# adaLN chunks of a two-layer diffusion block: transposes that end a chunk moved to later tiles, the steps of the first layer's chunks all on GpSimd, and the two value matmuls of a key tile made to wait for both their inputs

## The chip, the cores and the metric

The kernel runs on one core of one Trainium2 chip. The metric is the time of one execution on the device, in microseconds (us). Three timed runs of the kernel before gave 1271.01, 1266.54 and 1269.44 us, median 1269.44 us. One further execution was profiled, and all rows shown are from it.

## The reference, cut to what matters

Two layers work on 512 latent tokens of 1024 features (`h`); 256 context tokens feed the first layer's keys and values only. The first layer is windowed attention (16 heads of 64, 4 groups of keys and values, blocks of 128 queries, a sink per head), the second a short gated convolution. Each is followed by a feed-forward part (FFN) with a convolution over the tokens and 2816 hidden features. All is float32.

```
m = silu(c) @ ada_w[i] + ada_b[i]                 # (6 * 1024), per layer
sh1, sc1, g1, sh2, sc2, g2 = split(m, 6)
a = rms_norm(h) * (1 + sc1) + sh1
h = h + g1 * mixer(a)                             # layer 0: window attention, layer 1: gated conv
a = rms_norm(h) * (1 + sc2) + sh2
h = h + g2 * ((silu(conv(g)) * conv(u)) @ w_down) # g, u = split(a @ w_up, 2)
# attention, per head and block of 128 queries:
e = exp(s - max); o = (e @ v) / (sum(e) + exp(sink - max))
```

The six vectors of a layer are called chunks 0 to 5 here: shift, scale and gate of the mixer, then shift, scale and gate of the FFN.

## The kernel before, in words

Activations are held with features on the 128 rows, so `h` is 8 tiles of 128x512. Large products run as three matmuls in a reduced float32 format on a high and a low part of each operand (`mm3`, lines 168 to 171): each weight piece is loaded by SyncE's DMA queue (`wraw`, line 145), cast by ScalarE (line 137) and subtracted by VectorE (line 138).

**Order.** The code is written as one long sequence, and a scheduler that runs when the program is built turns it into one queue per engine (TensorE, VectorE, ScalarE, GpSimd) and one for SyncE's DMAs. It goes by the order of the code, but lets an instruction pass another one that it takes to be not yet ready; it works with its own estimates of durations. On the chip each queue is then worked off strictly in order. `tc.keep_in_program_order` keeps an instruction behind all that the code has put on its engine before it. Two hand-written lists give the order of the code: `START` up to the keys and values, `HEADS` for the attention.

**adaLN chunks.** Chunks 0 and 1 of layer 0 are computed at the start by TensorE. The others are computed in steps, `ada_step(layer, chunk, kt)`, off TensorE: a step loads 128 rows of `ada_w` as two halves of 128x512 (`araw`, 4 buffers) and adds them, times a column of silu(c), to two accumulators of 128x512 (`adaacc`, 2 buffers, the two halves of one chunk). After the eighth step (`kt` 7) the sum over the 128 rows is still to be taken: for each half, four transposes on TensorE into the bank `qt` (line 240), a reduction on VectorE (242) and the bias (243). In the attention the `a` steps of `HEADS` do chunks 2, 3, 4 of layer 0, one half of a step on VectorE (227, 229), the other on GpSimd (231, or 233 and 234). In layer 0's FFN, `tail0(j)` after each of the 22 tiles j does up to three steps, for chunk 5 of layer 0 and chunks 0 to 5 of layer 1, both halves on GpSimd.

**FFN of layer 0.** Tile j is two projections of 8 feature tiles (48 matmuls of 512 columns). After tiles 7, 15 and 21 the finished third is projected down (`out_proj`): 8 output tiles of 8, 8 or 6 hidden tiles, three matmuls each.

**Attention.** For a head and query block, `score` makes two or four matmuls, VectorE finds maxima and masks (line 552), ScalarE exponentiates (555). `value(p, j)` takes key tile j for the two heads of pair p: it transposes the weights of 2, 3 or 4 query blocks (583) into banks `pt` (3 of them), copies them out to `pf` (3 buffers; VectorE at 588 for context tiles, ScalarE at 590 for the others), and multiplies by the values (592). The even head's result goes to rows 0 to 63 of one bank, the odd head's to rows 64 to 127, each by its own matmul with 64 of the array's 128 columns; the profile lists each as two instructions. For key tiles 0 and 5, with two query blocks, both heads share one `pf` and one copy. `inverse_sums` (`r`) and `normalise` (`f`) finish a pair; the low part of the result is made on GpSimd (612).

GpSimd also adds the two halves of the rotary turn of keys and queries (line 435) and makes the scale of late queries (420, 421). Keys are transposed at line 467 once they are turned (430 to 435, 454).

Of the kernel before, what the change touches and what calls it, by code (L numbers as in the profile page):

```python
# [8 lines left out]
F32R = mybir.dt.float32r  # L9
AF = mybir.ActivationFunctionType  # L10
# [3 lines left out]
P = 128  # L14
T = 512
# [12 lines left out]
# Key tiles stand in the order lat0 lat1 ctx0 ctx1 lat2 lat3, so the keys of every query block are one window.  # L28
# [5 lines left out]
HOOK_AT = 6  # a norm's second half goes out after so many steps of the next phase's first group  # L34
HALF_AT = 2  # and its first half after so many tiles of the last phase's second half
KEY_BLOCKS = ((0, 2), (0, 3), (0, 4), (0, 4), (1, 4), (2, 4))

# Columns of the packed small parameters.
PC = {}
_n = 0  # L40
for _k, _w in (("c", 16), ("gmix", 16), ("adab", 2 * 6 * KT), ("gffn", 16), ("fconv", 2 * 3 * 2 * NF), ("sconv", 3 * KT),
# [6 lines left out]
# The order of the steps up to the keys and values: x, c, a, w, p load latents, context, a slice of ada_w, weights of k and v and the  # L48
# other parameters; r are the rstds, g a slice of silu(c) @ ada_w, s a split of weights, m and n the modulated features of latents and
# context, l and t their keys and values, k keeps the tensor engine's clock up while it waits.  # L50
# [4 lines left out]
# The order of the steps of the attention: q is a block of the second half of q, h the transposes of a pair of heads, s.b a head's scores  # L55
# of a query block, v.j a pair's values of a key tile, r its inverse sums, f its output, a a step of silu(c) @ ada_w, L and W weights.
HEADS = """
    q0 h0 a s0.0 s0.1 s0.3 s0.2 h1 s1.0 s1.1 s1.3 q2 a s1.2 s2.1 s2.3 s2.2 q1 v0.2 q3 v0.0 v0.3 s3.1 a h2 s2.0 a s3.0 s3.2 r0 v0.1
    a s3.3 v0.4 v0.5 f0 a s4.1 s4.0 s4.3 h3 v1.2 v1.3 a s4.2 s5.1 s5.0 a v1.0 s5.2 v1.1 s5.3 v1.4 v1.5 r1 a s6.0 s6.1 f1 s6.3 h4 a
    s6.2 v2.3 a v2.2 s7.0 a r2 s7.1 s7.3 s7.2 a v2.0 v2.1 v2.4 v2.5 s8.0 f2 a h5 s8.2 v3.3 s8.3 v3.0 s8.1 a s9.0 a s9.1 s9.3 v3.2  # L60
    v3.1 r3 a a s9.2 v3.4 s10.0 s10.1 s10.3 v3.5 s10.2 v4.2 f3 h6 v4.3 a v4.1 s11.0 s11.1 s11.3 s11.2 r4 s13.1 v4.0 v4.4 s12.3 a
    s12.2 a v4.5 f4 h7 a v5.3 v5.2 s12.0 s13.0 s12.1 a s13.3 v5.1 a v5.0 s13.2 v5.4 v5.5 r5 f5 s14.0 s14.3 s14.1 s14.2 L v6.2 v6.3
    s15.0 W s15.1 r6 s15.3 s15.2 v6.0 v6.1 v6.4 v6.5 v7.2 v7.3 v7.0 v7.1 r7 v7.4 f6 v7.5 f7
# [4 lines left out]
def kernel(ctx: ExitStack, tc: tile.TileContext, xT, ctxT, par_d, rope_d, mask_d, ident_d,  # L68
# [43 lines left out]
    # ---------------------------------------------------------------- constants  # L112
# [22 lines left out]
    # ---------------------------------------------------------------- helpers  # L135
# [12 lines left out]
    splits = [0, 0]  # so many splits in one piece, then so many in halves  # L148
# [33 lines left out]
    def rstd(acc, late=False, tag=None):  # L182
        """1 / sqrt(mean + EPS) of the tokens of acc (sums of squares by feature row), the same on all rows."""
        n = acc.shape[-1]
        nb = n // P
        ps = bank(tag) if tag else nbank()
        for b in range(nb):
            pe.matmul(out=ps[:, b:b + 1], lhsT=acc[:, b * P:(b + 1) * P], rhs=ones[:, 0:1], start=True, stop=True)
        c_ = small(NB, "rcol")[:, :nb]
        if late:  # L190
            vec.tensor_scalar(out=c_, in0=ps[:, :nb], scalar1=EPS, scalar2=None, op0=ALU.add)
            pool.tensor_tensor(out=c_, in0=c_, in1=mhalf[:, :nb], op=ALU.pow)
        else:
            act.activation(out=c_, in_=ps[:, :nb], func=AF.Sqrt, bias=epst, scale=1.0)
            vec.reciprocal(out=c_, in_=c_)
        ps = bank(tag) if tag else nbank()
        for b in range(nb):
            pe.transpose(out=ps[:, b * P:(b + 1) * P], in_=c_[:, b:b + 1].broadcast_to([P, P]), identity=ident)
        r = tmp()[:, :n]
        act.copy(out=r, in_=ps[:, :n])  # L200
        return r

    def modulate(x, r, s, sh, hi, lo):
        """hi + lo = x * s * r + sh."""
        n = tmp()[:, :x.shape[-1]]
        vec.scalar_tensor_tensor(out=n, in0=x, scalar=s, in1=r, op0=ALU.mult, op1=ALU.mult)
        act.activation(out=hi, in_=n, func=AF.Identity, scale=1.0, bias=sh)
        vec.scalar_tensor_tensor(out=lo, in0=n, scalar=sh, in1=hi.bitcast(F32), op0=ALU.add, op1=ALU.subtract)  # L208
# [3 lines left out]
    def ada_step(layer, ch, kt):  # L212
        """One of the KT steps of a chunk of silu(c) @ ada_w; the last one also leaves the chunk as columns."""
# [8 lines left out]
        for half in range(2):  # L222
            w, a = raws[half], acc[half]
            c_ = cs[:, kt, 0:1]
            if adastate["eng"][half] == "v":
                if kt == 0:
                    vec.tensor_scalar(out=a, in0=w, scalar1=c_, scalar2=None, op0=ALU.mult)
                else:
                    vec.scalar_tensor_tensor(out=a, in0=w, scalar=c_, in1=a, op0=ALU.mult, op1=ALU.add)
            elif kt == 0:  # L230
                pool.tensor_scalar(out=a, in0=w, scalar1=c_, scalar2=1.0, op0=ALU.mult, op1=ALU.mult)
            else:
                pool.tensor_scalar(out=w, in0=w, scalar1=c_, scalar2=1.0, op0=ALU.mult, op1=ALU.mult)  # L233
                pool.tensor_tensor(out=a, in0=a, in1=w, op=ALU.add)  # L234
        if kt < KT - 1:
            return
# [11 lines left out]
    # ---------------------------------------------------------------- layer 0: adaLN, norm, keys, values, queries  # L248
# [6 lines left out]
    with ExitStack() as attn:  # L255
# [22 lines left out]
        with tc.tile_pool(name="start", bufs=1, reuse_waits="tile") as st:  # L278
# [46 lines left out]
            def gemv(e):  # L325
                """Columns e*128.. of shift and scale for c and c_ctx: rows of partial sums side by side in the array, then columns."""
# [44 lines left out]
        adastate["eng"] = "vp"  # L371
        adastate["acc_alloc"] = lambda: ap.tile([P, 512], F32, tag="aacc", name=nm("adaacc"), bufs=2)
# [30 lines left out]
        def inv_rms(ss, out, scale, n):  # L403
            """out = scale / sqrt(ss / HD + EPS), the square root refined by one Newton step; n columns."""
# [10 lines left out]
        def inv_rms_late(ps, out):  # L415
            """Minus the above for 8 heads of q, without a change of the activation table."""
# [6 lines left out]
        def do_rope(src, tab, b, nh, out):  # L423
            """src [P, nh*HD] -> out, rotated by the gained tables of block b."""
# [33 lines left out]
        # keys transposed: KA holds k_hi on both halves of the rows, KB holds k_lo  # L458
# [46 lines left out]
        # ------------------------------------------------------------ window attention  # L505
# [9 lines left out]
        def head_pair(h):  # L515
            """q of heads h, h+1 transposed; each as a tile with q_hi on one half of the rows and q_lo on the other."""
# [15 lines left out]
        def score(h, b):  # L532
            """Unnormalised weights of head h for query block b; their sums go to den, after the last block the sinks' part to dsk."""
# [27 lines left out]
        def value(p, j):  # L561
            """Values of key tile j of heads 2p, 2p + 1, weighted, feature-major: the even head on rows 0.. of po, the odd on 64.."""
# [12 lines left out]
            for t in range(2):  # L575
# [9 lines left out]
                if t or not both:  # L585
                    w = 512 if both else n * P
                    if j in CTX_SLOT:
                        vec.tensor_copy(out=pf[:, :w], in_=pt[:, :w])
                    else:
                        act.copy(out=pf[:, :w], in_=pt[:, :w])  # L590
            for t in range(2):
                pe.matmul(out=po[t * HD:(t + 1) * HD, b0 * P:b1 * P], lhsT=V[:, j, kv, :], rhs=pfs[t], start=first, stop=not pair["left"])  # L592

        def inverse_sums(p):
            """1 / (den + dsk) of a pair of heads, spread over the rows of their values."""
# [4 lines left out]
            inv = ap.tile([P, 512], F32, tag="inv", name=nm("inv"), bufs=1)  # L600
# [3 lines left out]
            R = pairs[p]["R"] = ap.tile([P, 512], F32, tag="R", name=nm("R"), bufs=2)  # L604
# [9 lines left out]
        adastate["eng"] = "vp"  # L614
        for step in HEADS.split():
# [14 lines left out]
            elif k == "a":  # L630
                ada_step(*asteps.pop(0))
# [6 lines left out]
    # ---------------------------------------------------------------- the rest, feature-major  # L638
    with tc.tile_pool(name="ffn", bufs=1, reuse_waits="tile") as fp, three_banks() as sp3:
# [5 lines left out]
        adastate["acc_alloc"] = lambda: fp.tile([P, 512], F32, tag="aacc", name=nm("adaacc"), bufs=2)  # L645
# [10 lines left out]
        def proj(pieces, ah, al, halves=False, group=None, hook=None):  # L656
            """One bank for each weight piece; k-major over `group` pieces at a time. `hook` is called HOOK_AT steps in."""
# [37 lines left out]
        def out_proj(src, n, ah, al, gate, nxt=None, last=False, lead=(), tail_w=None):  # L695
            """h += gate * (W^T a). With `nxt`, h is final after it and the next norm follows half by half."""
# [33 lines left out]
        adastate["eng"] = "pp"  # L730
# [35 lines left out]
        fsteps = [(0, 5, kt) for kt in range(KT)] + [(1, ch, kt) for ch in range(6) for kt in range(KT)]  # L766

        def tail0(j):
            for _ in range(3 if j else 0):
                if fsteps:  # L770
                    ada_step(*fsteps.pop(0))

        def after_ffn0():
            assert not fsteps
# [7 lines left out]
        # layer 1: short gated convolution  # L782
# [88 lines left out]
```

## Time and profile before

| what | value |
|---|---|
| timed runs | 1271.01, 1266.54, 1269.44 us; median 1269.44 |
| profiled execution | span 1263.3 us; its own full time is not given, the median is 6.1 us above its span |
| TensorE busy | 1227.5 us, 97% |
| VectorE, ScalarE, GpSimd busy | 772.6, 490.3, 352.5 us |
| mean granted TensorE clock | 0.991 |
| start, to about 118 us | keys, values, first queries |
| attention | about 118 to 275 us |
| output projection and norm | about 275 to 325 us |
| FFN of layer 0 | about 325 to 682 us |
| layer 1 | about 682 to 1263 us |

How rows are read: DVE is VectorE, ACT ScalarE, POOL GpSimd, SP SyncE, PE a matmul and PEld the load of its weights. A row of a view names engine, line, operation, what is written from what is read, and a count. A row of a list of waits says how long an engine sat idle before instructions of a line, and whose end released it. In a timeline the columns are start and length in us, and in brackets the idle time before. Matmuls overlap: the time from one matmul's start to the next one's start tells more than a duration. A transpose is a matmul too.

### The profile page before, as it was taken

The page shows a single profiled execution, that of the slowest core. Times are in us where ns is not written, and L with a number is a line of the kernel's source. Part 1 is how long each engine was busy: PE and PEld are TensorE (multiplying, and loading weights), DVE is VectorE, ACT ScalarE, POOL GpSimd, SP SyncE. Part 2 cuts the span into 40 slices and gives each one's busy share as a digit, 9 for nine tenths or more (in the row PEclk, how much of TensorE's full clock was granted, in tenths as well). Part 3 has the DMA queues.
Part 4 walks back from the last instruction along what each step waited for, and adds up shares of the span by engine and source line. Part 5 has one row for each costly group of instructions (what it writes and reads, how often), then busy time and mean ns, then how long its engine had stood idle before and what let it go on. Part 6 is the DMA issues. An engine that isn't in the chain of part 4 may idle for free.

```text
span 1263.3 us, 16133 instructions
## 1 busy us (share of the span) xinstructions
PE 1227.5 (97%) x6190; PEld 986.5 (78%) x6190; DVE 772.6 (61%) x1157; ACT 490.3 (39%) x812; POOL 352.5 (28%) x301
## 2 busy tenths in 40 slices
PE   8989999999899999989999999999999999999998
PEld 6667655568887788777878998888988888888888
DVE  4789878735887637765575764443676436653652
ACT  4435666642463223331234442332454224432330
POOL 0054344209329928897280100001000000000000
PEclk8989999999999999989999999999999999999999
DMA  9454232035344554555342233222233233323211
GB/s 366 168 184 158 68 125 85 25 112 196 109 146 151 202 168 151 200 193 193 120 149 96 89 113 100 89 96 83 68 133 98 87 99 100 100 87 98 80 38 67
DMA packets 57741, 157.58 MB, mean 125 GB/s; under 512 B 6464, under 2 KB 8000, under 8 KB 57664
## 3 DMA queue, kind: packets, MB, share of 16 engines
q1 hardware_dynamic: 57664, 156.56, 37.6%
q8 instruction: 48, 0.79, 0.3%
q14 instruction: 29, 0.24, 0.1%
HBM read 152.86 MB, written 2.10 MB: 123 GB/s over the span
## 4 chain that ended last, share of the span: by engine, by line
PE 77%; POOL 13%; DVE 5%; issue 2%; DMA 1%; ACT 1%; SPq 0%; POOLq 0%; DVEq 0%; ACTq 0%
PE ps_s L170 8%; PE ps_s L169 8%; PE ps_s L171 8%; PE ps_pt L170 7%; PE ps_pt L171 7%; POOL adaacc L234 7%; PE ps_pt L169 7%; POOL araw L233 5%; PE ps_oa L592 5%; PE ps_oa L170 3%; PE ps_oa L169 3%; PE ps_oa L171 3%; PE ps_pt L583 3%; PE ps_qt L170 2%; PE ps_qt L171 2%; PE ps_qt L169 2%
## 5 line engine op out<-in xcount | busy, mean ns | idle before, releaser
L138 DVE TENSOR_TENSOR wlo<-wraw,whi 128x1024 fp32r<-128x1024 f32 (+2 forms) x206 | 246.0, 1202 | 165.1 <-ACT whi L137 160.3
L137 ACT CAST whi<-wraw 128x1024 fp32r<-128x1024 f32 (+2 forms) x206 | 195.9, 959 | 332.8 <-PE ps_s L170 98.6
L234 POOL TENSOR_TENSOR adaacc<-adaacc,araw 128x512 f32<-128x512 f32 x119 | 171.9, 1451 | 6.3
L170 PE MATMUL ps_s<-a,whi 128*128 128x512 f32 (+1 forms) x376 | 140.5, 374 | 2.6 <-DVE a L208 2.6
L169 PE MATMUL ps_s<-a,whi 128*128 128x512 f32 (+1 forms) x376 | 140.6, 374 | 0.0
L171 PE MATMUL ps_s<-a,wlo 128*128 128x512 f32 (+1 forms) x376 | 140.0, 372 | 0.0
L169 PE MATMUL ps_pt<-a,whi 128*128 128x512 f32 (+1 forms) x368 | 135.8, 369 | 0.0
L170 PE MATMUL ps_pt<-a,whi 128*128 128x512 f32 (+1 forms) x368 | 135.7, 369 | 0.0
L171 PE MATMUL ps_pt<-a,wlo 128*128 128x512 f32 (+1 forms) x368 | 135.1, 367 | 0.0
L233 POOL TENSOR_SCALAR araw<-araw,cs 128x512 f32<-128x512 f32 x119 | 117.7, 993 | 45.2 <-DMA araw<-in_ada 40.1
L137 ACT CAST g<-f 128x512 fp32r<-128x512 f32 x52 | 32.2, 620 | 141.4 <-DVE f L754 140.8
L170 PEld LDWEIGHTS ps_s<-a,whi 128*128 128x128 f32 x376 | 71.3, 190 | 14.8 <-DVE a L208 2.8
L169 PEld LDWEIGHTS ps_s<-a,whi 128*128 128x128 f32 x376 | 71.3, 190 | 12.3
L171 PEld LDWEIGHTS ps_s<-a,wlo 128*128 128x128 f32 x376 | 71.2, 189 | 12.2
L169 PE MATMUL ps_pt<-g,whi 128*128 128x512 f32 (+1 forms) x222 | 78.3, 353 | 1.2 <-ACT g L137 0.6
L169 PEld LDWEIGHTS ps_pt<-a,whi 128*128 128x128 f32 x368 | 69.8, 190 | 11.3
L171 PEld LDWEIGHTS ps_pt<-a,wlo 128*128 128x128 f32 x368 | 69.7, 189 | 11.1
L170 PE MATMUL ps_pt<-g,whi 128*128 128x512 f32 (+1 forms) x222 | 78.0, 352 | 0.2 <-DVE g L138 0.2
L170 PEld LDWEIGHTS ps_pt<-a,whi 128*128 128x128 f32 x368 | 69.7, 189 | 10.8
L171 PE MATMUL ps_pt<-g,wlo 128*128 128x512 f32 (+1 forms) x222 | 78.0, 352 | 0.0
L171 PE MATMUL ps_s<-g,wlo 128*128 128x512 f32 (+1 forms) x222 | 77.9, 352 | 0.0
L169 PE MATMUL ps_s<-g,whi 128*128 128x512 f32 (+1 forms) x222 | 77.7, 351 | 0.0
(258 smaller groups left out, 2489.7 us busy)
## 6 DMA issues: line engine op xcount, KB each, us to landing
wraw<-in_wup SPq DMA_DIRECT2D x88, 512.0 KB, 3.6
araw<-in_ada SPq DMA_DIRECT2D x160, 256.0 KB, 2.9
wraw<-in_wdown SPq DMA_DIRECT2D x32, 512.0 KB, 3.9
wraw<-in_wsc SPq DMA_DIRECT2D x24, 512.0 KB, 3.6
gw<-in_ada SPq DMA_DIRECT2D x16, 512.0 KB, 9.9
wraw<-in_wqkv SPq DMA_DIRECT2D x12, 512.0 KB, 6.8
wraw<-in_wdown SPq DMA_DIRECT2D x16, 384.0 KB, 3.2
wraw<-in_wo SPq DMA_DIRECT2D x8, 512.0 KB, 4.0
```

Source lines behind the costliest of these rows:

```text
L137: act.copy(out=hi, in_=raw)
L138: vec.tensor_tensor(out=lo, in0=raw, in1=hi.bitcast(F32), op=ALU.subtract)
L169: pe.matmul(out=ps, lhsT=wh, rhs=ah, start=start, stop=False)
L170: pe.matmul(out=ps, lhsT=wh, rhs=al, start=False, stop=False)
L171: pe.matmul(out=ps, lhsT=wl, rhs=ah, start=False, stop=stop)
L233: pool.tensor_scalar(out=w, in0=w, scalar1=c_, scalar2=1.0, op0=ALU.mult, op1=ALU.mult)
L234: pool.tensor_tensor(out=a, in0=a, in1=w, op=ALU.add)
L583: pe.transpose(out=pt[:, q:q + P], in_=heads[2 * p + t]["e"][b][:, o:o + P], identity=ident)
L592: pe.matmul(out=po[t * HD:(t + 1) * HD, b0 * P:b1 * P], lhsT=V[:, j, kv, :], rhs=pfs[t], start=first, stop=not pair["left"])
```

## The change

- `ada_step` no longer ends a chunk. The transposes, reduction and bias are a function of their own, `ada_cols`, called later: in `HEADS` at three new `A` steps, in the FFN after tiles 5, 8, 11, 14, 17, 19 and 21. The steps themselves stay where they were in the code, and apart from the `A` steps `HEADS` is the same sequence.
- All halves of all steps go to GpSimd. The first instruction of the first step is kept in program order.
- `adaacc` has 4 buffers in place of 2, in both places. To make room in the attention, `inverse_sums` takes a general buffer in place of its own `inv`, and `R` has one buffer in place of two.
- Layer 1's chunks are computed in the order 1, 0, 4, 3, 2, 5.
- In `value`, where the heads have a copy each, the even head's matmul also waits for the odd head's copy.

```diff
+DEP = mybir.DependencyInfo(mybir.DependencyClass.Sync, mybir.DependencyReason.DATA)
+COLS_AT = (5, 8, 11, 14, 17, 19, 21)
 HEADS (only the new steps and their neighbours):
-    ... s7.0 a r2 ...          +    ... s7.0 a A r2 ...
-    ... s12.3 a s12.2 ...      +    ... s12.3 a A s12.2 ...
-    ... v7.0 v7.1 r7 ...       +    ... v7.0 A v7.1 r7 ...
...
-    def ada_step(layer, ch, kt):
+    def ada_step(layer, ch, kt, pin=False):
...
-            if adastate["eng"][half] == "v":
-                if kt == 0:
-                    vec.tensor_scalar(out=a, in0=w, scalar1=c_, scalar2=None, op0=ALU.mult)
-                else:
-                    vec.scalar_tensor_tensor(out=a, in0=w, scalar=c_, in1=a, op0=ALU.mult, op1=ALU.add)
-            elif kt == 0:
-                pool.tensor_scalar(out=a, in0=w, scalar1=c_, scalar2=1.0, op0=ALU.mult, op1=ALU.mult)
+            if kt == 0:
+                ins = pool.tensor_scalar(out=a, in0=w, scalar1=c_, scalar2=1.0, op0=ALU.mult, op1=ALU.mult)
+                if pin and half == 0:
+                    tc.keep_in_program_order(ins)
             else:
                 pool.tensor_scalar(out=w, in0=w, scalar1=c_, scalar2=1.0, op0=ALU.mult, op1=ALU.mult)
                 pool.tensor_tensor(out=a, in0=a, in1=w, op=ALU.add)
-        if kt < KT - 1:
-            return
+        if kt == KT - 1:
+            adadone.append((layer, ch, acc))
+
+    adadone = []
+
+    def ada_cols():
+        layer, ch, acc = adadone.pop(0)
         for half in range(2):
             ps = bank("qt")
...
-        adastate["acc_alloc"] = lambda: ap.tile([P, 512], F32, tag="aacc", name=nm("adaacc"), bufs=2)
+        adastate["acc_alloc"] = lambda: ap.tile([P, 512], F32, tag="aacc", name=nm("adaacc"), bufs=4)
...
-                        vec.tensor_copy(out=pf[:, :w], in_=pt[:, :w])
+                        landed = vec.tensor_copy(out=pf[:, :w], in_=pt[:, :w])
                     else:
-                        act.copy(out=pf[:, :w], in_=pt[:, :w])
+                        landed = act.copy(out=pf[:, :w], in_=pt[:, :w])
             for t in range(2):
-                pe.matmul(out=po[t * HD:(t + 1) * HD, b0 * P:b1 * P], lhsT=V[:, j, kv, :], rhs=pfs[t], start=first, stop=not pair["left"])
+                mm = pe.matmul(out=po[t * HD:(t + 1) * HD, b0 * P:b1 * P], lhsT=V[:, j, kv, :], rhs=pfs[t], start=first, stop=not pair["left"])
+                if t == 0 and not both:
+                    tc.add_manual_dep(mm.ins, landed.ins.name, DEP, reason="both heads at once")
...
-            inv = ap.tile([P, 512], F32, tag="inv", name=nm("inv"), bufs=1)
+            inv = tmp()
...
-            R = pairs[p]["R"] = ap.tile([P, 512], F32, tag="R", name=nm("R"), bufs=2)
+            R = pairs[p]["R"] = ap.tile([P, 512], F32, tag="R", name=nm("R"), bufs=1)
...
-                ada_step(*asteps.pop(0))
+                ada_step(*asteps.pop(0), pin=len(asteps) == 23)
+            elif k == "A":
+                ada_cols()
...
-        adastate["acc_alloc"] = lambda: fp.tile([P, 512], F32, tag="aacc", name=nm("adaacc"), bufs=2)
+        adastate["acc_alloc"] = lambda: fp.tile([P, 512], F32, tag="aacc", name=nm("adaacc"), bufs=4)
...
-        fsteps = [(0, 5, kt) for kt in range(KT)] + [(1, ch, kt) for ch in range(6) for kt in range(KT)]
+        fsteps = [(0, 5, kt) for kt in range(KT)] + [(1, ch, kt) for ch in (1, 0, 4, 3, 2, 5) for kt in range(KT)]
...
                 if fsteps:
                     ada_step(*fsteps.pop(0))
+            if j in COLS_AT:
+                ada_cols()
```

More of the change, by code (lines that the diff above doesn't have):

```diff
@@ L57 @@
 HEADS = """
[L58 to L63, printed above, removed]
+    q0 h0 a s0.0 s0.1 s0.3 s0.2 h1 s1.0 s1.1 s1.3 q2 a s1.2 s2.1 s2.3 s2.2 q1 v0.2 q3 v0.0 v0.3 s3.1 a h2 s2.0 a s3.0 s3.2 r0 v0.1 a
+    s3.3 v0.4 v0.5 f0 a s4.1 s4.0 s4.3 h3 v1.2 v1.3 a s4.2 s5.1 s5.0 a v1.0 s5.2 v1.1 s5.3 v1.4 v1.5 r1 a s6.0 s6.1 f1 s6.3 h4 a s6.2
+    v2.3 a v2.2 s7.0 a A r2 s7.1 s7.3 s7.2 a v2.0 v2.1 v2.4 v2.5 s8.0 f2 a h5 s8.2 v3.3 s8.3 v3.0 s8.1 a s9.0 a s9.1 s9.3 v3.2 v3.1 r3
+    a a s9.2 v3.4 s10.0 s10.1 s10.3 v3.5 s10.2 v4.2 f3 h6 v4.3 a v4.1 s11.0 s11.1 s11.3 s11.2 r4 s13.1 v4.0 v4.4 s12.3 a A s12.2 a v4.5
+    f4 h7 a v5.3 v5.2 s12.0 s13.0 s12.1 a s13.3 v5.1 a v5.0 s13.2 v5.4 v5.5 r5 f5 s14.0 s14.3 s14.1 s14.2 L v6.2 v6.3 s15.0 W s15.1 r6
+    s15.3 s15.2 v6.0 v6.1 v6.4 v6.5 v7.2 v7.3 v7.0 A v7.1 r7 v7.4 f6 v7.5 f7
 """
@@ L370 @@
         adastate["raw"] = lambda: ap.tile([P, 512], F32, tag="araw", name=nm("araw"), bufs=4)
-        adastate["eng"] = "vp"
-        adastate["acc_alloc"] = lambda: ap.tile([P, 512], F32, tag="aacc", name=nm("adaacc"), bufs=2)
+        adastate["acc_alloc"] = lambda: ap.tile([P, 512], F32, tag="aacc", name=nm("adaacc"), bufs=4)
         asteps = [(0, ch, kt) for ch in (2, 3, 4) for kt in range(KT)]
@@ L612, in normalise @@
             pool.tensor_tensor(out=o_lo[p], in0=on, in1=o_hi[p].bitcast(F32), op=ALU.subtract)
-        adastate["eng"] = "vp"
         for step in HEADS.split():
@@ L729 @@
         lead_tail = [wpiece(None, 1024, raw) for raw in lead_raw]
-        adastate["eng"] = "pp"
         scale_cols(smod[:, 2, :], ada[0][:, 4, :], pc("gffn", 0, 8))
@@ L771, in tail0 @@
                     ada_step(*fsteps.pop(0))
+            if j in COLS_AT:
+                ada_cols()
         def after_ffn0():
-            assert not fsteps
+            assert not fsteps and not adadone
             scale_cols(smod[:, 3, :], ada[1][:, 1, :], pc("gmix", 8, 8))
```

## The prediction

> **What bounds the kernel now.** I read the page first, then the waits of TensorE, then the stages by windows, then the timeline of TensorE where the change acts. First the busy times, the granted clock by slices, and TensorE's and GpSimd's waits:
>
> ```profile
> PE 1227.5 (97%) x6190; PEld 986.5 (78%) x6190; DVE 772.6 (61%) x1157; ACT 490.3 (39%) x812; POOL 352.5 (28%) x301
> PEclk8989999999999999989999999999999999999999
> ...
> POOL adaacc L231 <- PE ps_qt L240: 99.1, 4, 41.7
> ...
> PE ps_qt L240 <- POOL adaacc L234: 10.2, 4, 4.4
> PE ps_pt L467 <- DVE e L454: 5.2, 2, 4.3
> PE ps_s L170 <- DVE a L208: 2.6, 1, 2.6
> ```
>
> TensorE sets the end: 97% busy. What can be won is its idle time, time at a lower granted clock, and array time used badly. Two of its longest waits are touched. The largest is the chunk-ending transposes waiting for GpSimd, yet GpSimd waits 99.1 us for those same transposes: with two accumulators it stands still until a chunk is transposed, then runs a chunk flat out with TensorE close behind. The timeline of TensorE (and one row of GpSimd) shows it:
>
> ```profile
> 372.15 0.70 POOL L231 TENSOR_SCALAR adaacc<-araw,cs 128x512 f32<-128x512 f32 x1 [41.70 <-PE ps_qt L240]
> ...
> 407.43 0.65 PE L240 MATMUL ps_qt<-ident,adaacc 128*128 128x128 f32 x4 [2.09 <-POOL adaacc L234]
> ...
> 551.62 1.12 PE L240 MATMUL ps_qt<-ident,adaacc 128*128 128x128 f32 x4 [4.38 <-POOL adaacc L234]
> ...
> 556.94 0.39 PE L169 MATMUL ps_s<-a,whi 128*128 128x512 f32 x1
> 557.17 0.40 PE L170 MATMUL ps_s<-a,whi 128*128 128x512 f32 x1
> ```
>
> Windows, whose columns are the stretch, its length, busy time of PE, PEld, DVE, ACT and POOL with counts, the granted clock and DMA:
>
> ```profile
> 81.40:88.00 6.60, 1.39 (x7) 0.86 (x7) 6.60 (x11) 1.23 (x4) 5.62 (x6) 0.81 0.12 40
> 88.00:92.40 4.40, 4.40 (x12) 3.45 (x11) 4.34 (x9) 2.15 (x5) 2.60 (x3) 0.50 0.60 164
> ...
> 512.20:515.60 3.40, 3.40 (x13) 2.81 (x12) 2.90 (x5) 0.00 (x0) 1.53 (x2) 0.50 0.62 180
> ...
> 549.80:556.60 6.80, 4.99 (x16) 4.20 (x17) 3.82 (x7) 0.00 (x0) 4.18 (x5) 0.50 0.59 190
> ...
> 118.00:275.00 157.00, 155.93 (x800) 92.43 (x799) 117.50 (x240) 100.31 (x233) 51.80 (x47) 1.00 0.23 73
> ```
>
> So idle stretches are followed by half clock: near 88, 512 and 552 us. The last row is the attention: TensorE is busy throughout, VectorE 75%, ScalarE 64%.
>
> **The FFN's transposes.** The 10.2 us go if GpSimd ends each chunk before its new place. A matmul takes 0.23 us (556.94 to 557.17), so a tile's 48 take 11.0 us and a projection down after tile 7 or 15 (192) takes 44. The transposes at 371.5, just before GpSimd's row at 372.15, are those after tile 3; from there the new places come at about 393 (tile 5), 470 (8), 503 (11), 536 (14), 613 (17), 635 (19) and 657 (21). GpSimd needs 407.43 - 372.15 = 35.3 us for a chunk in one go. With four accumulators chunk n waits only for the transposes of chunk n - 2. The first chunk is done before GpSimd's 41.70 us of idling, at 330; then 366, 429 (from 393), 505 (from 470), 541, 577 and 648 (from 613). Each is ahead of its place, the tightest by 9 us (648 against 657). So I take the whole **-10.2 us**; bounds -10.2 and 0, for the same chase at new places. The work that hides GpSimd is then two tiles of matmuls; without it, each us late is a us lost. The number of transposes is unchanged. The new order of chunks brings the columns wanted first at layer 1's start earlier and costs nothing.
>
> **The clock behind those waits.** Half clock lasts 3.40 us in one stretch, all of it at work: half is lost, 1.7 us. In the other, 4.99 us of work lose 2.5. Together **-4.2 us**, bounds -4.2 and 0. The Trainium skill, page "TensorE: Matmul & The Clock Gate", part "The HAM clock gate", has the array fall to half clock after an idle window of about 3.4 us. By that only the 4.38 us wait would have cost anything, and the term would be -2.5; the trace lowers the clock near 512 too, where no wait reached 3.4, so the rows decide.
>
> **Value matmuls.** The groups of line 592 by shape, and pieces of TensorE's timeline:
>
> ```profile
> L592 PE MATMUL ps_oa<-pf,V 128*64 128x512 f32 x64 | 28.2, 617 | 0.8 <-DVE pf L588 0.6
> L592 PE MATMUL ps_oa<-pf,V 128*64 128x384 f32 x64 | 25.9, 509 | 0.1
> ...
> L592 PE MATMUL ps_oa<-pf,V 128*64 128x256 f32 x64 | 13.6, 404 | 0.2
> ```
> ```profile
> 242.91 0.65 PE L592 MATMUL ps_oa<-pf,V 128*64 128x256 f32 x4
> ...
> 245.62 1.07 PE L592 MATMUL ps_oa<-pf,V 128*64 128x512 f32 x2
> 246.62 0.66 PE L583 MATMUL ps_pt<-ident,e 128*128 128x128 f32 x4
> ...
> 249.21 1.08 PE L592 MATMUL ps_oa<-pf,V 128*64 128x512 f32 x4
> 250.22 0.88 PE L583 MATMUL ps_pt<-ident,e 128*128 128x128 f32 x6
> ...
> 251.46 0.65 PE L592 MATMUL ps_oa<-pf,V 128*64 128x256 f32 x2
> ...
> 253.65 0.86 PE L592 MATMUL ps_oa<-pf,V 128*64 128x384 f32 x2
> ```
>
> One head's matmul (two instructions) of 512 columns holds TensorE from 245.62 to 246.62, 1.00 us; both heads' back to back (249.21, x4) take 1.01. The two halves of the array work at once, and the second is free if it follows directly. Today most don't follow: 16 such key tiles cost 28.2 us where 16 x 1.08 = 17.3 would do, 16 of 384 columns cost 25.9 where 16 x 0.86 = 13.8 would do (the pair taken as long as the one at 253.65, as at 512). That is 23.0 us, or 21 without the tails of 0.07 us (1.07 against 1.00) that some 25 parted rows already share with what follows. After the change both become ready with one copy. How often the scheduler then keeps them together shows in the tiles that always had one copy: 13.6 us, where 16 pairs like 242.91 would take 10.4 and all parted 20.8, so 69% are together (251.46 is parted). 0.69 x 21 = **-14 us**; bounds -21 and 0.
>
> The added wait can cost. Behind the even head's matmul in TensorE's queue stand transposes and scores, and for these VectorE and ScalarE. Only three `pf` buffers exist, so a held pair lets just one more copy land. Today that wait shows as 0.6 us (row of line 592 <- DVE). With 14 us less, the stage is 143 us of TensorE against 117.5 - 13 of VectorE and 100 of ScalarE, 73% and 70%: near enough to lose some. I take **+3 us**, bounds 0 and +8 (the second copy late by 0.25 us, a third of a copy, in each of 32 tiles).
>
> **VectorE's halves to GpSimd.** By shape, in the attention and (last row) before it:
>
> ```profile
> L229 DVE SCALAR_TENSOR_TENSOR adaacc<-araw,cs,adaacc 128x512 f32<-128x512 f32 x16 | 12.9, 807 | 0.1
> L234 POOL TENSOR_TENSOR adaacc<-adaacc,araw 128x512 f32<-128x512 f32 x15 | 19.9, 1327 | 1.3
> L233 POOL TENSOR_SCALAR araw<-araw,cs 128x512 f32<-128x512 f32 x14 | 10.6, 759 | 24.5 <-DMA araw<-in_ada 19.4 <-PE ps_pt L583 3.7 <-DVE nmx L552 1.3
> ...
> 113.48 1.29 POOL L435 TENSOR_TENSOR qr<-t,t 128x512 f32<-128x512 f32 x1
> ```
>
> VectorE loses 13 us in the attention, which is off the path and counted in the 73% above. GpSimd's half step is 1.33 + 0.76 = 2.09 us, so 48 halves are at most 100 us. The pin puts the first behind the addition at 113.48. GpSimd's other work there is 51.8 - 19.9 - 10.6 = 21 us, so it ends near 113 + 121 = 234, ahead of the last `A` step, half way through the last pair, some 255 by then. SyncE's queue waits for the same buffers at the same pace. Cost nothing, cover 20 us. `inv`, `R` and the general buffer: a pair's `R` is written after the pair before is normalised, since both pairs' results share one bank; nothing.
>
> **The start.** Before 118 us the same steps stand in the way of the keys. Timelines of VectorE and TensorE:
>
> ```profile
> 70.17 0.86 DVE L229 SCALAR_TENSOR_TENSOR adaacc<-araw,cs,adaacc 128x512 f32<-128x512 f32 x1
> ...
> 72.92 1.45 DVE L229 SCALAR_TENSOR_TENSOR adaacc<-araw,cs,adaacc 128x512 f32<-128x512 f32 x1
> ...
> 78.39 0.49 DVE L433 TENSOR_TENSOR t<-e,tabk 128x128 f32<-128x128 f32 x2
> ...
> 82.36 2.07 DVE L433 TENSOR_TENSOR t<-e,tabk 128x128 f32<-128x128 f32 x2
> ...
> 86.03 0.48 PE L467 MATMUL ps_pt<-ident,e 128*128 128x128 f32 x1 [4.28 <-DVE e L454]
> ```
>
> VectorE works without a pause to 87 us, and TensorE waits 5.2 us for the last keys, then loses half of 4.40 us to the clock: 7.4 to be had. VectorE's own ada rows here are 2.3 us (0.86 and 1.45), and GpSimd's beside it stretch others: a pair of line 433 took 2.07 us at 82.36 against 0.49 at 78.39. The pin holds GpSimd's first half back; the other half's first steps may still go early, until the four load buffers are held. I take **-5 us**, bounds -7.4 and +2 (those steps in the keys' way on GpSimd's own queue).
>
> **The norm before the FFN.** GpSimd's second chunk now runs from 330 to 366, over the norm's second half, where it idled. In the first half, with GpSimd at work, TensorE waited 2.6 us (line 170 <- DVE a). I take **+1**, bounds 0 and +2.6.
>
> **Sum.** -10.2 - 4.2 - 14 + 3 - 5 + 1 = -29.4 us; span 1263.3 - 29.4 = 1233.9; with the 6.1 us by which the median of the runs lies above the span, **1240 us**, 2.3% faster.
>
> **Rivals.**
> *The pairs don't form.* TensorE's queue is fixed at build by estimates, and it may part the heads as it parts 31% of the tiles with one copy. Then -14 is 0: 1254 us. For it: row 251.46. Against it: 242.91.
> *The chase moves.* The tightest margin is 9 us over six 35 us chunks; if the scheduler puts transposes ahead of the chip again, the FFN's 14.4 us come back: 1254 us. Against it: a place is never earlier than its tile.
> *GpSimd becomes the bound of the attention; slower.* All 24 steps now run on one engine. A step of two halves is 4.2 us; its slowest rows are the FFN's 35.3 / 8 = 4.4, but there it shares with other work. TensorE stands at the last `A` step if GpSimd ends after 255; all gain is gone when it ends 29 us later, at a step of (284 - 113 - 21) / 24 = 6.3 us. At 7 us, a stretch like the 1.45 against 0.81 that VectorE's own row suffers, it ends at 302: 1240 + 47 = about 1287 us. Against it: GpSimd's rows in the attention are no slower than 1327 and 759 ns on average beside a VectorE that is 75% busy. The Trainium skill, page "SBUF — State Buffer", section "Who interferes with whom", has a VectorE instruction with two SBUF inputs block a GpSimd instruction that reads SBUF, for its whole length; it speaks against doing this on GpSimd, and by it the attention's mostly PSUM-fed VectorE work would block little, as the rows have it.
> *It does little.* The scheduler's other order eats what each part gives: within 4 us of now, 1268.
>
> **How the numbers follow.** Forecast 0.65, pairs 0.12, chase 0.10, GpSimd bound 0.09, little 0.04. Faster 0.65 + 0.12 + 0.10 = 0.87; same 0.04; slower 0.09 (0.3% is about what a measurement of this kernel can tell from none). With every bound at its best (-10.2 - 4.2 - 21 - 7.4) it is 1227; the forecast's own range is 1227 to 1252. The two weaker cases reach 1254 and, with +8 in place of +3, 1259; so 1226 to 1260.
>
> **What would show it.** Right: no wait of line 240 for GpSimd over 1 us in the FFN and full clock from 400 to 680; line 592's 512 and 384 groups at 33 to 42 us in place of 54; the wait of line 467 under 2 us. Wrong: a wait of TensorE for GpSimd in the attention, or line 592 unchanged.

## The result

The changed kernel takes 1281.8 us (median of 4 runs, 1281.3 to 1282.5) against 1269.2 us before on the same chip: a ratio of 1.010, 95% interval 1.008 to 1.012. It is **1% slower**; the forecast was 1240 us, 2.3% faster. Its profiled span is 1279.5 us, 16.2 more than before. The medians differ by 12.6 us: a run of the changed kernel takes 1.8 us more than its own span, so by the same 1.8 the profiled execution of before (span 1263.3) took some 1265 us, less than any of its timed runs.

The page of the changed kernel hardly differs in its totals. TensorE's busy time has even fallen by 3 us:

```profile
PE 1224.6 (96%) x6190; PEld 989.8 (77%) x6190; DVE 771.0 (60%) x1133; ACT 491.6 (38%) x812; POOL 387.3 (30%) x346
...
PEclk8999699999789999998999999999999999999999
```

The loss has to be looked for by stages. The table is worked out from the timelines of both kernels: from the first score matmul to the last value matmul is the attention, from there to the first up-projection matmul (line 169 before, 172 after) the output projection, on to the first up-projection matmul of 512 columns the norm, on to tile 21's gate product the FFN's rest. The norm's stage holds all the work of tiles 0 and 1, which are computed in two token halves of 256 columns; it is what the expectations below mean by the way from the first FFN matmul "to the second half". The last column is a version made below.

| stage, us | before | after | change | best version |
|---|---|---|---|---|
| to the first score | 112.9 | 105.5 | -7.4 | 106.5 |
| attention | 161.7 | 173.0 | +11.3 | 152.7 |
| output projection | 48.5 | 49.9 | +1.4 | 50.4 |
| norm and first group (tiles 0 and 1) | 26.7 | 41.9 | +15.2 | 27.7 |
| rest of the FFN's tiles | 334.7 | 329.1 | -5.6 | 329.3 |
| last projection down and layer 1 | 578.9 | 580.1 | +1.2 | 578.6 |

The waits of TensorE in the changed kernel show that the two that the prediction read are gone: the transposes (now line 246) wait 0.8 us, for VectorE, and the keys (line 472) wait 0.6 us.

```profile
PE ps_oa L597 <- DVE t L438: 11.3, 1, 11.3
PE ps_pt L172 <- ACT g L140: 8.1, 2, 7.1
PE ps_s L173 <- DVE a L211: 5.4, 4, 2.3
PE ps_pt L588 <- DVE t L438: 5.2, 1, 5.2
PE ps_pt L191 <- DVE f L183: 3.7, 1, 3.7
...
PE ps_qt L246 <- DVE ada L248: 0.8, 1, 0.8
...
PE ps_pt L472 <- DVE KB L478: 0.6, 1, 0.6
```

In their place stand new ones. Four windows of the changed kernel, and then the norm's window of the kernel before (columns: stretch, length, busy time of PE, PEld, DVE, ACT, POOL with counts, granted clock, DMA share and GB/s):

```profile
118.00:150.00 32.00, 15.44 (x69) 10.52 (x67) 13.59 (x24) 7.91 (x13) 31.50 (x31) 0.75 0.37 114
...
328.40:370.20 41.80, 30.99 (x199) 29.60 (x198) 38.11 (x40) 10.63 (x23) 37.07 (x34) 0.80 0.50 164
```
```profile
345.80:359.40 13.60, 10.25 (x45) 9.66 (x46) 12.42 (x14) 2.16 (x5) 13.27 (x13) 0.50 0.51 167
584.70:591.50 6.80, 4.43 (x10) 3.43 (x11) 4.61 (x5) 1.66 (x2) 6.80 (x6) 0.50 0.37 116
```
```profile
323.00:349.50 26.50, 23.89 (x199) 23.63 (x198) 18.86 (x41) 10.08 (x23) 4.44 (x4) 1.00 0.29 100
```

From 118 to 150 us, in the attention, TensorE works 15.44 us, VectorE 13.59, ScalarE 7.91; only GpSimd is busy throughout. In the norm GpSimd is busy for 37.07 us where it had 4.44, and VectorE needs 38.11 us for some 40 instructions that took 18.86 before.

**The attention.** The chain is read backwards: TensorE's row, then VectorE's rows, then GpSimd's:

```profile
135.77 1.98 PE L597 MATMUL ps_oa<-pf,V 128*64 128x512 f32 x4 [11.35 <-DVE t L438]
```
```profile
123.81 0.23 DVE L424 TENSOR_SCALAR ss<-ss 128x8 f32<-128x8 f32 x1
134.86 0.76 DVE L438 TENSOR_TENSOR t<-ps_oa,tabq 128x256 f32<-128x256 f32 x2 [10.83 <-POOL qr L440]
```
```profile
106.13 1.29 POOL L440 TENSOR_TENSOR qr<-t,t 128x512 f32<-128x512 f32 x1
107.39 1.38 POOL L229 TENSOR_SCALAR adaacc<-araw,cs 128x512 f32<-128x512 f32 x2
...
128.67 1.26 POOL L234 TENSOR_TENSOR adaacc<-adaacc,araw 128x512 f32<-128x512 f32 x1
129.89 1.65 POOL L425 TENSOR_TENSOR ss<-ss,mhalf 128x8 f32<-128x8 f32 x1
...
133.57 1.26 POOL L440 TENSOR_TENSOR qr<-t,t 128x512 f32<-128x512 f32 x1
```

A late q block's rotary turn leaves two products in general buffers `t` (four of them), and GpSimd's addition (line 440) sets them free. From 107.39 to 129.89 GpSimd works through 23 instructions of adaLN steps before it comes to the next q block's scale and addition. VectorE's products of the block after that find no free buffer and wait 10.83 us; the value matmul waits for a bank that those products still read, 11.35 us. A second time, at 150 us, TensorE waits 5.2.

**The norm.** Three modulations of the same shape, before and after:

```profile
336.43 1.28 DVE L206 SCALAR_TENSOR_TENSOR t<-h,smod,t 128x256 f32<-128x256 f32 x3 [0.93 <-ACT t L200]
```
```profile
351.27 3.66 DVE L209 SCALAR_TENSOR_TENSOR t<-h,smod,t 128x256 f32<-128x256 f32 x3 [1.18 <-ACT t L203]
```

The three take 2.9 times as long beside GpSimd's second chunk (3.66 us against 1.28).

### The profile page after: what moved, and what is told of

The parts are those of the page before. It is cut to its first block, busy times and chain, and to the rows that moved or that the text cites. A ratio compares the mean times of both kernels' runs of the same rounds, so it can differ in the third digit from the quotient of the medians.

```text
span 1279.5 us, 16116 instructions
## 1 busy us (share of the span) xinstructions
PE 1224.6 (96%) x6190; PEld 989.8 (77%) x6190; DVE 771.0 (60%) x1133; ACT 491.6 (38%) x812; POOL 387.3 (30%) x346
## 4 chain that ended last, share of the span: by engine, by line
PE 75%; POOL 10%; DVE 9%; issue 3%; DMA 2%; ACT 1%; SPq 0%; POOLq 0%; DVEq 0%; ACTq 0%
PE ps_s L173 8%; PE ps_s L172 8%; PE ps_s L174 8%; PE ps_pt L174 8%; PE ps_pt L173 8%; PE ps_pt L172 8%; POOL adaacc L234 5%; PE ps_oa L597 4%; POOL araw L233 3%; PE ps_oa L174 2%; PE ps_oa L173 2%; PE ps_oa L172 2%; PE ps_qt L173 2%; PE ps_qt L174 2%; PE ps_qt L172 2%
## 5 line engine op out<-in xcount | busy, mean ns | idle before, releaser
L141 DVE TENSOR_TENSOR wlo<-wraw,whi 128x1024 fp32r<-128x1024 f32 (+2 forms) x206 | 249.9, 1221 | 175.9 <-ACT whi L140 171.2
L234 POOL TENSOR_TENSOR adaacc<-adaacc,araw 128x512 f32<-128x512 f32 x140 | 197.8, 1421 | 6.8
L233 POOL TENSOR_SCALAR araw<-araw,cs 128x512 f32<-128x512 f32 x140 | 130.8, 939 | 21.9 <-DMA araw<-in_ada 21.6
```

Source lines behind the costliest of these rows:

```text
L141: vec.tensor_tensor(out=lo, in0=raw, in1=hi.bitcast(F32), op=ALU.subtract)
```

## The experiments

The theory after the first look: the parts do what was predicted, and what loses is work that now stands behind GpSimd's steps: VectorE's rotary products in the attention, VectorE's modulations in the norm, the weight loads in SyncE's queue at tile 15. The main rival in the attention: the wait added in `value`, or GpSimd's load as such. Times before are 1265.7 to 1266.2 us in these comparisons; a ratio is always to the kernel before on the same chip.

### The added wait alone

The kernel before, and of the change only this:

```
-                        vec.tensor_copy(out=pf[:, :w], in_=pt[:, :w])
+                        landed = vec.tensor_copy(out=pf[:, :w], in_=pt[:, :w])
...
+                if t == 0 and not both:
+                    tc.add_manual_dep(mm.ins, landed.ins.name, DEP, reason="both heads at once")
```

> The kernel before with the added wait in `value` alone. Theory: that part works as predicted and the loss of the whole change lies elsewhere; both heads' value matmuls pair up, their start-to-start sum falls from 59.8 to about 48 us, and the time from 1269 to about 1257 us. Rival: the added wait gives back what the pairs win, or is itself what stops TensorE in the attention; then the attention's TensorE shows new waits of 10 us or more in all and the time stays at 1266 or above.

Measured: 1257.5 us, ratio 0.992 (0.989 to 0.994). The attention falls from 161.7 to 151.5 us; from each value matmul's start to the next start on TensorE, all summed, it is 45.6 us against 59.8 (47.9 in the changed kernel). The wait of its value matmuls is now

```profile
PE ps_oa L593 <- DVE pf L589: 2.2, 3, 0.9
```

So this part gains 10 us where it acts, and the wait in `value` is not what stopped TensorE. Some 5 us of the gain do not arrive: from the last value matmul to the FFN it takes 53.6 us in place of 48.5. Why was not followed up.

### VectorE's halves undone, and the queue's order alone

First, the changed kernel with VectorE doing the first halves of the attention's steps again (the one instruction kept in program order is then GpSimd's first):

```
+            if adastate["eng"][half] == "v":
+                if kt == 0:
+                    vec.tensor_scalar(out=a, in0=w, scalar1=c_, scalar2=None, op0=ALU.mult)
+                else:
+                    vec.scalar_tensor_tensor(out=a, in0=w, scalar=c_, in1=a, op0=ALU.mult, op1=ALU.add)
+            elif kt == 0:
```

> The changed kernel with one part undone: in the attention VectorE does the first half of every adaLN step again, GpSimd the second, as before. Theory (the late q blocks' rotary additions stand behind too many half steps in GpSimd's queue, and VectorE behind them): TensorE's waits for VectorE's rotary product (11.3 and 5.2 us) go, the attention falls from 173.0 to about 150 us, the time from 1282 to some 1259 us, at most 7 us more where VectorE's halves come back ahead of the keys. Rival (the loss comes from the wait in `value`, or from four accumulators): the waits stay and the time is 1278 or above.

Measured: 1271.0 us, ratio 1.003 (1.001 to 1.005); attention 160.4 us. That is between the two expectations. Half of the steps are still in GpSimd's queue ahead of the addition, and the chain is still there, shorter:

```profile
DVE t L444 <- POOL qr L446: 5.6, 1, 5.6
...
PE ps_oa L603 <- DVE pf L599: 5.0, 1, 5.0
```

Second, all halves stay on GpSimd, but their multiplications may not go ahead of what the code has before them:

```
-                if pin and half == 0:
+                if pin:
...
+                if pin:
+                    tc.keep_in_program_order(ins)
...
-                ada_step(*asteps.pop(0), pin=len(asteps) == 23)
+                ada_step(*asteps.pop(0), pin=True)
```

> The changed kernel with all 24 steps of the attention on GpSimd as there, but each of their multiplications kept in program order, so that no half step goes ahead of a rotary addition that the code has before it. Theory (the order of GpSimd's queue is the cause, not its load): the waits for VectorE's rotary product go or fall under 2 us, the attention is about 150 us in place of 173.0, and the time about 1258 us. Rival (GpSimd has too much work for the attention): TensorE waits for GpSimd at the last transposes of a chunk, by 8 us or more, or VectorE is still held by the rotary additions, and the time is 1275 or above.

Measured: 1259.5 us, ratio 0.994 (0.992 to 0.996). The attention takes 152.7 us, 20.3 less than in the changed kernel, with the same work on GpSimd. The window that had 15.44 us of TensorE, and GpSimd's rows:

```profile
118.00:150.00 32.00, 30.38 (x168) 19.92 (x166) 29.39 (x56) 21.37 (x43) 30.50 (x28) 1.00 0.37 123
```
```profile
107.76 1.37 POOL L229 TENSOR_SCALAR adaacc<-araw,cs 128x512 f32<-128x512 f32 x2
118.26 1.65 POOL L427 TENSOR_TENSOR ss<-ss,mhalf 128x8 f32<-128x8 f32 x1 [9.13 <-DVE ss L426]
120.00 0.21 POOL L428 TENSOR_SCALAR nrq<-ss 128x8 f32<-128x8 f32 x1
120.16 1.28 POOL L442 TENSOR_TENSOR qr<-t,t 128x512 f32<-128x512 f32 x1
```

GpSimd now idles 9.13 us ahead of the q block, and the addition that came at 133.57 comes at 120.16. It is still busy for 30.50 of the 32 us (31.50 in the changed kernel): its load was not the cause, the order of its queue was. At the transposes that end a chunk, TensorE never waits for GpSimd in the attention.

### The norm, with the second chunk held back

On the changed kernel, the first instruction of the FFN's second chunk waits for the gate product of tile 1:

```
+                if after is not None and half == 0:
+                    tc.add_manual_dep(ins.ins, after.ins.name, DEP, reason="behind the first tiles")
...
+                    ada_step(*fsteps.pop(0), after=prod[1] if len(fsteps) == 47 else None)
```

> The changed kernel, with the first instruction of the FFN's second adaLN chunk on GpSimd held back until VectorE has done the gate product of the FFN's second tile; nothing else is different. Theory (GpSimd's chunk over the norm stretches VectorE's and ScalarE's way through modulation and splits): from the first FFN matmul to the second half takes 26 to 30 us in place of 41.8, the half clock from 346 to 359 goes, and the time falls from 1282 to about 1268 us. Rival (the norm is late for another reason, such as the new order of the queues or the residuals before it): that stretch stays above 36 us and the time within 4 us of 1282.

Measured: 1285.7 us, ratio 1.015 (1.011 to 1.019). The stage behaves as the theory said, 27.9 us in place of 41.9, but the time does not (1268 was expected): between tiles 2 and 5 TensorE gets a new wait.

```profile
420.87 1.09 PE L248 MATMUL ps_qt<-ident,adaacc 128*128 128x128 f32 x4 [16.78 <-DVE f L686]
```

The same hold, placed earlier (behind the norm's last modulation), on the kernel with the attention in program order:

> The kernel with the attention's steps kept in program order (1259.5 us), with the FFN's second adaLN chunk held behind the last modulation of the norm's second half, so 14 us or more earlier than the hold tried on the changed kernel. Theory (the hold heals the norm, and what it costs is SyncE's queue, in which weight loads stand behind the held chunk's loads): first FFN matmul to second half about 28 us in place of 42.0, a new wait in tiles 2 to 5 of at most 5 us with its half clock, and about 1248 to 1254 us. Rival (the earlier hold lost its time because the transposes at tile 5 were then too early for GpSimd): no wait of TensorE for weights or splits in those tiles, but at least 8 us at the transposes after tile 5.

Measured: 1260.1 us, ratio 0.994 (0.993 to 0.996), the same as without the hold. The norm takes 25.1 us, the rest of the tiles 342.8 in place of 329.1. The expected stall of at most 5 us and time of 1248 to 1254 us were wrong: the stall is 13.1 us. Its windows, and the rows of SyncE's queue and of the waits there:

```profile
309.00:334.00 25.00, 23.90 (x199) 23.64 (x198) 17.24 (x40) 9.47 (x22) 9.33 (x10) 1.00 0.43 147
...
384.00:400.00 16.00, 5.07 (x19) 4.34 (x20) 12.00 (x16) 5.81 (x8) 3.51 (x4) 0.57 0.40 123
```
```profile
336.13 23.58 SPq L222 DMA_DIRECT2D araw<-in_ada  x10
359.81 0.37 SPq L148 DMA_DIRECT2D wraw<-in_wup  x1
```
```profile
ACT whi L140 <- DMA wraw<-in_wup: 17.7, 2, 15.3
...
PE ps_qt L252 <- DVE f L690: 13.1, 1, 13.1
```
```profile
POOL adaacc L231 <- PE ps_qt L252: 29.2, 2, 29.0
```

SyncE spends 23.58 us on ten loads for the chunk, which wait for GpSimd to free their buffers; the next weights stand behind them. ScalarE waits 15.3 us for those weights; VectorE's convolutions fall behind, and at the transposes after tile 5 TensorE waits 13.1 us for a bank that one of them still reads (line 690). So the wait stands where the rival put it. But GpSimd was not late: its next chunk waits 29.0 us for these transposes, and it is nearly idle while they wait (3.51 of 16 us). That the late weights began this is read from the order of the rows and not tested alone. In the norm's window the DMA share is 0.43, against 0.29 in the kernel before, and the norm is as short as there: the transfers as such do not slow it.

### The FFN's loads on GpSimd's own queue

`sp.dma_start` becomes `pool.dma_start` for the steps of the FFN; first with the norm as it is, then with the earlier hold.

> The kernel with the attention's steps kept in program order (1259.5 us), with the FFN's adaLN loads issued from GpSimd's own queue in place of SyncE's. Theory (the 7.4 us wait of TensorE after tile 15 is a weight load that stands in SyncE's queue behind loads waiting for GpSimd's buffers): that wait and its 6.8 us of half clock go, and the time falls to about 1249 us; the norm stays at 42 us. Rival (the split or the gate product before the projection down is late by VectorE's own work): the wait stays above 5 us and the time within 3 us of 1259.5.

> Both: the second chunk held behind the norm, and the FFN's adaLN loads on GpSimd's own queue, on the kernel with the attention's steps in program order (1259.5 us). Theory (what is queued behind GpSimd's steps is all that is wrong with the changed kernel): norm stage about 28 us (14 less), the wait after tile 15 and its half clock gone (10.8 less), no stall in tiles 2 to 5: about 1236 us. Rival (GpSimd's loads or its share of the memory ports cost as much as the queue did): 1248 us or above.

Measured: ratios of 1.004 (1.001 to 1.006; runs of 1264.3 to 1278.0 us) and 0.993 (0.991 to 0.996; 1258.9 us). The first is slower than the 1259.5 us that it started from, where 1249 was expected; no profile of it is used here, and the reason is not shown. In the second, the wait after tile 15 is 1.8 us, where the same kernel with these loads on SyncE's queue has 7.1, and the norm took 23.8 us, as the theory of SyncE's queue has it. The time came back elsewhere: the tiles from 2 on took 337.3 us in place of 329.1, which was not followed up, and the output projection before the FFN 61.5 us in place of 50.3. Two rows of its waits say why the projection did:

```profile
DVE f L183 <- POOL f L183: 12.3, 1, 12.3
...
PE ps_pt L172 <- DVE h L701: 8.3, 2, 7.3
```

GpSimd's first sums of squares for the norm now stood behind the FFN's first chunk in GpSimd's queue; VectorE waited 12.3 us for them, and TensorE 7.3 us for VectorE. The 1236 us that I expected were wrong by 23: the third queue had the same fault.

### The FFN's part undone, and its transposes late again

On the kernel with the attention in program order: two accumulators in the FFN, transposes right behind each chunk, chunks in the old order.

> The kernel with the attention's steps kept in program order (1259.5 us), with the FFN's part of the change undone: two accumulators, transposes right behind each chunk's last step, chunks in the old order. Theory (the FFN's part as a whole loses, because it moves a chunk over the norm and leaves SyncE's weight loads behind its own): first FFN matmul to second half falls from 42.0 to about 27 us and the 7.4 us wait for the first weights of the projection down, with its half clock, goes, against 14 us of waits and half clock at the transposes that come back; about 1248 us. Rival (the FFN's part gains its predicted 14.4 us net and the norm is slow for what happens in the attention): 1270 us or above.

Measured: 1252.5 us (1250.9 to 1255.5), ratio 0.988 (0.986 to 0.991). The norm is back at 27.9 us, the waits at transposes too:

```profile
PE ps_qt L248 <- POOL adaacc L236: 10.0, 4, 4.4
```

So the FFN's part, as it was made, cost about 7 us net (1259.5 against 1252.5). Then, with two accumulators and the old order of chunks kept, only the transposes were moved. Shown against the changed kernel:

```
-COLS_AT = (5, 8, 11, 14, 17, 19, 21)
+COLS_AT = (3, 7, 8, 12, 15, 16, 20)
...
-        adastate["acc_alloc"] = lambda: fp.tile([P, 512], F32, tag="aacc", name=nm("adaacc"), bufs=4)
+        adastate["acc_alloc"] = lambda: fp.tile([P, 512], F32, tag="aacc", name=nm("adaacc"), bufs=2)
```

> The kernel with the attention's steps kept in program order and the FFN's part undone (1252.5 us), with one piece of the FFN's part put back: a chunk's transposes stand after a later tile (3, 7, 8, 12, 15, 16, 20), at least 40 us apart, while two accumulators keep GpSimd's second chunk behind the first transposes and so out of the norm. Theory (late transposes are right as predicted, and the loss is only in running ahead over the norm and SyncE's queue): the waits of TensorE for GpSimd at transposes (10.0 us) and the half clock at 500 and 537 us go, first FFN matmul to second half stays near 28 us, no wait over 2 us after tile 15; about 1240 us. Rival (GpSimd's or SyncE's queue is late again at the new places): a wait of 4 us or more at a transpose or at the first weights of a projection down, and 1248 us or above.

Measured: **1245.3 us** (1244.1 to 1247.0), ratio 0.983 (0.981 to 0.986): faster than both kernels, and 7 of the 12 us that I expected against the run before.

```profile
PE ps_qt L248 <- POOL adaacc L236: 3.0, 2, 1.7
...
PE ps_pt L172 <- ACT g L140: 1.9, 1, 1.9
PE ps_qt L248 <- DVE ada L250: 1.9, 1, 1.9
```

The waits for GpSimd fall from 10.0 to 3.0 us; 1.9 us each for VectorE's reduction and for the split before the projection down take some of it back. The norm stays at 27.7 us.

Last, the same kernel with VectorE's first halves, kept in program order on both engines:

> The kernel with transposes after tiles 3, 7, 8, 12, 15, 16 and 20 and two accumulators in the FFN, in which VectorE does the first half of each of the attention's steps again, all of them kept in program order on both engines. Theory (once the queue's order is right, which engine does the halves is off the path, as the term of nothing said): within 4 us of the same kernel with all halves on GpSimd. Rival (the halves on GpSimd are worth something of their own, or hold VectorE by the memory's ports): at least 5 us away from it, to either side, in the attention's windows.

Measured: 1251.4 us, ratio 0.988 (0.986 to 0.991); attention 162.0 us against 152.7. So it is 6 us slower, and the theory's 4 us bound fell. But the added wait alone, with VectorE's halves in the order that the scheduler chose, had 151.5 us. This run changes the engine and VectorE's order together, and the kernel with the added wait alone also has the old buffers and places of the transposes; which of these costs the 9 us was not tried.

## Why the prediction was wrong

**Value matmuls: right.** -14 was predicted, 59.8 - 47.9 = -11.9 us measured. The share of pairs that stay together was also right, though not evenly: by TensorE's order in the changed kernel, 15 of the 16 key tiles with 512 columns are together, but only about 7 of the 16 with 384, in all 22 of 32 or 69%. The price of the added wait (+3) is in line with the 2.2 us that the value matmuls wait in the kernel with that part alone. The attention gains 10.2 us from it in that kernel. The groups of the value matmuls in the changed kernel, by shape, are 41.2 us for the two wide shapes, within the 33 to 42 named in the prediction:

```profile
L597 PE MATMUL ps_oa<-pf,V 128*64 128x384 f32 x64 | 21.3, 511 | 0.0
L597 PE MATMUL ps_oa<-pf,V 128*64 128x512 f32 x64 | 19.9, 669 | 12.0 <-DVE t L438 11.3 <-DVE pf L593 0.6
```

**The start: right in size, and only in part for the reason given.** -5 predicted, with -7.4 as the best; -7.4 measured. The version in which VectorE does the first halves again still has three of its rows on accumulators ahead of 90 us (2.25 us), and comes to the first score at 105.6 us all the same. None of GpSimd's rows on accumulators is there, where the kernel before has 7.81 us of them. So VectorE's own rows cost nothing here. That keeping GpSimd's halves back made the gain is the likely reading; it was not tried alone.

**The FFN's transposes: right at their places.** The waits for GpSimd went from 10.2 us to none, and the half clock at 512 and 550 us went too. Full clock from 400 to 680 us, the other sign named, did not come: it is half from 584.70 to 591.50, for another reason (below). The best version shows that later transposes are worth having, if GpSimd does not run ahead.

**"Cost nothing, cover 20 us": the step that failed.** The working asked whether GpSimd has time enough, and it does: its last half step ends at 218 us, where 234 was predicted, and TensorE waits at no chunk-ending transpose in the attention. It did not ask what else is in GpSimd's queue. It named SyncE and the `A` steps as those who wait for GpSimd, and left out the rotary additions, though the row of one (line 435) was quoted just above. The scheduler lets an instruction pass another that it takes to be not ready, so the steps went ahead of the additions; behind the additions stood VectorE, through the four general buffers, and behind VectorE TensorE. The price was 20.3 us (173.0 against 152.7), shown by order alone. Of the rivals, "GpSimd becomes the bound of the attention" had the engine and the sign, but not the mechanism: GpSimd did not end late. That its 1287 us lies near the measured 1281.8 is luck. The sign that the prediction named for being wrong, a wait of TensorE for GpSimd in the attention, came with VectorE's name on it; only the wait of VectorE behind it names GpSimd. `inv` and `R`, also put at nothing, were not tried alone; with them as changed the attention can take 152.7 us, against 151.5 in the kernel with the added wait alone, which leaves little for them.

**The norm, "+1, bounds 0 and +2.6": mis-sized.** That the second chunk would run over the norm was predicted; it cost 15.2 us. I priced it by one wait of 2.6 us in a stretch where GpSimd worked only part of the time. The trace of before had a better row: VectorE's modulations take 0.43 us each while GpSimd idles (the row at 336.43), and every feature tile of the norm passes through such two-input instructions. The Trainium skill, page "SBUF — State Buffer", section "Who interferes with whom", says that a VectorE instruction with two SBUF inputs contends with a GpSimd instruction that reads SBUF. This trace agrees, and adds who pays: three of VectorE's took 3.66 us in place of 1.28, while GpSimd's 34 instructions in that stage took 37.07 us, 1.09 us each, hardly more than the 1.05 of the prediction's half step (two instructions, 2.09 us). The prediction had used that section only for the attention, and for GpSimd as the one that is blocked; the section leaves it to the order of issue which of the two waits. That the second chunk is the cause is shown by the versions that keep it out of the norm: 27.9, 25.1 and 27.9 us.

**"SyncE's queue waits for the same buffers at the same pace": said of the attention, and left out for the FFN.** The sum for the FFN does not ask what stands behind the adaLN loads in SyncE's queue. With GpSimd running without a pause, SyncE stands at adaLN loads, and the first weights of the projection down come late. Two rows of the changed kernel:

```profile
564.92 7.20 SPq L220 DMA_DIRECT2D araw<-in_ada  x4
```
```profile
567.39 1.06 ACT L140 CAST whi<-wraw 128x1024 fp32r<-128x1024 f32 x1 [3.50 <-DMA wraw<-in_wdown]
```

ScalarE's split of the last gate product comes after such weights, and TensorE waits 7.1 us for it, until 587 us, with half clock from 584.70 to 591.50. The fall of that wait to 1.8 us with the loads off SyncE's queue supports this.

Together: the FFN's rest gained 5.6 us where 14.4 were predicted. The new wait took 7.1 of it, and half clock over 4.43 us of work another 2.2.

The sum also added 6.1 us between span and median. By the runs only 1.8 us lie between an execution and its own span; the other 4.3 are scatter between the runs of before, too little to change the outcome.

## What to carry to other kernels

When work is moved to an idle engine, free time is not the question; list every other instruction in that engine's queue, and who holds buffers until it has run. An engine that no longer has to wait will run ahead: find out what it then runs beside, and whose loads its own loads stand in front of. If waits are wanted for order, an ordering constraint costs less than the queue it prevents: here one left GpSimd idle for 9 us and won 20 us.

## What was not expected of the hardware

Half clock outlasts the wait that starts it by far when short waits follow. From 345.80 to 359.40 the granted clock was 0.50 although TensorE was busy for 10.25 of the 13.60 us; the idle times there are 3.72, 1.68 and 1.29 us:

```profile
346.18 1.01 PE L191 MATMUL ps_pt<-ones,f 128*128 128x1 f32 x4 [3.72 <-DVE f L183]
350.15 0.69 PE L201 MATMUL ps_qt<-ident,rcol 128*128 128x128 f32 x2 [1.68 <-DVE rcol L198]
356.39 0.58 PE L173 MATMUL ps_s<-a,whi 128*128 128x256 f32 x1 [1.29 <-DVE a L211]
```

The Trainium skill, page "TensorE: Matmul & The Clock Gate", part "The HAM clock gate", asks for about 3.4 us of sustained work before full clock returns; the trace agrees as far as waits of 1.29 and 1.68 us were enough to keep it down. But it shows more than that figure: from 350.15 to 355.10 TensorE works for 4.95 us with no idle time in its rows, and the clock stays at half.

In the norm, a GpSimd that is busy for 37.07 of 41.80 us beside VectorE's two-input work made these VectorE instructions 2.9 times as long (3.66 us against 1.28) and its own hardly longer (1.09 us against 1.05), which makes an adaLN step on GpSimd dearer for its neighbours than its own duration says.
